# Feed-forward gate in seven products of quarters for each pair of blocks, on one Trainium2 core

## The chip, the cores and the metric

The kernel runs on one core of a Trainium2 chip, as one program. Its metric is the device time in microseconds of one execution, the median over repeated runs. Five engines work beside each other, each through its own instructions in order: TensorE (PE; its weight loads are listed as PEld), VectorE (DVE), ScalarE (ACT), GpSimd (POOL) and SyncE (SP), which issues the loads. They wait for each other by semaphores.

## What is computed

Two transformer layers (a mixer, an attention to a memory, a gated feed-forward) and then one hybrid layer, for 256 tokens of 2048 features, in float32. The change is in the feed-forward, which both of the first two layers run, with 5632 hidden features:

```python
def swiglu(h, w_gate, w_up, w_down):
    return (jax.nn.silu(h @ w_gate) * (h @ w_up)) @ w_down
...
        h = rms_norm(x, ffn_norm_g[l])
        x = x + swiglu(h, w_gate[l], w_up[l], w_down[l]).astype(x.dtype)
```

Beside the second layer's feed-forward the kernel sums w_ada, the weights that the hybrid layer's shift, scale and gate come from (`ada = c @ w_ada + b_ada`, one row c).

## The kernel before

Every long product keeps float32 precision by splitting both operands into a high and a low part: high·high + high·low + low·high, three matmuls on TensorE in place of one. The activations are split once and kept, as four pairs (xh, xl) of 512 features by 256 tokens. The weights come from DRAM in blocks of 128 x 1024 (512 KB: two chunks of 128 input features by 512 columns). For each, SyncE issues the load into one of five buffers `raw` (L410), ScalarE copies it to `wh` (L411, the high part), and VectorE subtracts that to give `wl` (L412). `wh` and `wl` have four buffers each (pool `wp`). These three instructions have a high priority, so the scheduler puts them ahead of other work of their engines, as early as buffers allow.

`block` (L401 and on) makes 256 tokens by 512 columns of a product: two PSUM banks `pw`, one for each half (m) of the tokens, out of four. A weight block serves twelve matmuls of 512 columns: two chunks, two halves of the tokens, three parts (L423 to L425). For the last weight block the products of the second half are held back until those of the first are done, so the first bank is finished earlier. TensorE's order is the order in which the program is written; that of the other engines comes from the scheduler. Other work (transposes of what comes next, attention heads) is cut into tasks, and `tick`, called between matmuls, lets each go on by a step.

The feed-forward (`ffn`) goes over 11 blocks of 512 hidden features. `hidden(j)` makes the gate block (L1186, 96 matmuls, then silu on ScalarE from the banks, L1188), the up block (96 matmuls), multiplies the two on VectorE (L1192), and spawns the task that transposes the result (L377) and splits it (L358, L359). `down(j - 1)` then multiplies the block before with w_down: four blocks of 24 matmuls, each added to the residual x by VectorE (L485, twice 512 columns). In layer two, `ada(9)` runs after each block: nine loads of w_ada (L1239) and nine multiply-and-sum instructions of 1024 columns on VectorE (L1240).

## Time and profile before

| | before |
|---|---|
| median of 3 runs | 3197.86 us (3197.11 to 3198.05) |
| span of the profiled execution, first to last instruction | 3196.7 us |
| TensorE busy in that span | 3175.3 us |
| VectorE busy | 2034.1 us |
| ScalarE busy | 1553.8 us |
| feed-forward of layer one, from the first issue of w_gate on | 428.7 us |
| feed-forward of layer two, last issue of w_down | 2340.1 us |

A busy TensorE row means that matmuls follow each other without a gap, since a matmul's end overlaps with the next one's start: the distance between starts is what one costs. Busy times of VectorE overlap in the same way by about a tenth of a microsecond when its instructions follow closely. An engine's share over the span is a mean over stages that differ, so the windows by stage count more than the page's first part.

### The profile page before, as it was taken

What the parts mean: (1) busy time and instruction counts of PE and PEld (TensorE: products, weight loads), DVE (VectorE), ACT (ScalarE), POOL (GpSimd) and SP (SyncE); (2) the same over time, 40 slices, a digit from 0 to 9 for tenths busy, and PEclk for the clock granted to TensorE, in tenths of its full rate; (3) what the DMA queues carried; (4) which work ended last, traced back from release to release, by engine and by line L of the source; (5) the groups of instructions that cost most, each with busy time, mean ns of one, the idle gap of its engine ahead of it and who ended that gap; (6) DMA issues with size and microseconds to landing.
All of it is one profiled execution on the core that took longest, in us unless ns stands there. A gap on an engine that the chain in (4) does not pass through costs nothing.

```text
span 3196.7 us, 41513 instructions
## 1 busy us (share of the span) xinstructions
PE 3175.3 (99%) x15705; PEld 2656.9 (83%) x15705; DVE 2034.1 (64%) x3015; ACT 1553.8 (49%) x2191; POOL 53.4 (2%) x77
## 2 busy tenths in 40 slices
PE   9999999999999999999999999999999999999998
PEld 8987888888888889887888888888878977888887
DVE  6886665555555566885767677766765555455554
ACT  7465564444444455474654444444454455444443
POOL 0010000000000000010000000000000000000000
PEclk9999999999999999999999999999999999999999
DMA  8554555555555556454567777777746533555454
GB/s 299 172 169 145 186 172 187 192 192 191 192 187 192 191 175 189 159 183 141 190 228 265 266 270 270 253 250 269 269 143 219 174 105 99 179 184 180 162 184 151
DMA packets 175160, 625.28 MB, mean 196 GB/s; under 512 B 19696, under 2 KB 19952, under 8 KB 174704
## 3 DMA queue, kind: packets, MB, share of 16 engines
q1 hardware_dynamic: 173952, 620.26, 58.2%
q8 instruction: 123, 2.02, 0.3%
q10 hardware_dynamic: 1008, 2.37, 0.2%
q14 instruction: 77, 0.63, 0.1%
HBM read 620.46 MB, written 2.10 MB: 195 GB/s over the span
## 4 chain that ended last, share of the span: by engine, by line
PE 96%; DVE 1%; DMA 1%; issue 1%; POOL 0%; ACT 0%; SPq 0%; DVEq 0%; POOLq 0%; ACTq 0%
PE pw L423 27%; PE pw L425 27%; PE pw L424 27%; PE pw L461 2%; PE pw L462 2%; PE pw L463 2%; PE mb L377 2%; PE mb L665 2%; DMA wada<-w_ada 1%; PE mb L1493 1%; PE mb L1346 0%; PE mb L903 0%; DVE wl L412 0%; PE mb L1496 0%; PE mb L887 0%
## 5 line engine op out<-in xcount | busy, mean ns | idle before, releaser
L412 DVE TENSOR_TENSOR wl<-raw,wh 128x1024 fp32r<-128x1024 f32 (+3 forms) x1069 | 1285.6, 1204 | 969.7 <-ACT wh L411 967.2
L411 ACT ACTIVATE wh<-raw 128x1024 fp32r<-128x1024 f32 (+3 forms) x1069 | 1114.9, 1043 | 1384.8 <-PE pw L425 1258.0
L423 PE MATMUL pw<-wh,xh 128*128 128x512 f32 (+2 forms) x3952 | 1555.4, 394 | 6.2 <-ACT wh L411 4.9
L425 PE MATMUL pw<-wh,xl 128*128 128x512 f32 (+2 forms) x3952 | 1526.3, 386 | 0.0
L424 PE MATMUL pw<-wl,xh 128*128 128x512 f32 (+2 forms) x3952 | 1524.6, 386 | 0.6 <-DVE wl L412 0.6
L423 PEld LDWEIGHTS pw<-wh,xh 128*128 128x128 f32 x3952 | 744.2, 188 | 153.3 <-ACT wh L411 4.9
L425 PEld LDWEIGHTS pw<-wh,xl 128*128 128x128 f32 x3952 | 743.1, 188 | 150.7 <-DVE xl L368 0.7
L424 PEld LDWEIGHTS pw<-wl,xh 128*128 128x128 f32 x3952 | 744.6, 188 | 141.6 <-DVE wl L412 2.1
L461 PE MATMUL pw<-xh,wh 128*128 128x256 f32 x640 | 183.2, 286 | 0.0
L463 PE MATMUL pw<-xh,wl 128*128 128x256 f32 x640 | 181.2, 283 | 0.0
L462 PE MATMUL pw<-xl,wh 128*128 128x256 f32 x640 | 181.1, 283 | 0.0
L485 DVE TENSOR_TENSOR x<-x,pw 128x512 f32<-128x512 f32 x224 | 144.9, 679 | 3.8 <-PE pw L425 3.8
L1240 DVE CUSTOM_DVE_ANT_0 wada<-wada,crow 128x1024 f32<-128x1024 f32 x96 | 117.3, 1221 | 33.9 <-DMA wada<-w_ada 33.8
L461 PEld LDWEIGHTS pw<-xh,wh 128*128 128x128 f32 x640 | 122.7, 192 | 1.3 <-issue 0.8
L462 PEld LDWEIGHTS pw<-xl,wh 128*128 128x128 f32 x640 | 122.8, 192 | 0.1
L463 PEld LDWEIGHTS pw<-xh,wl 128*128 128x128 f32 x640 | 122.7, 192 | 0.0
L630 ACT ACTIVATE t<-t,mn 128x256 f32<-128x256 f32 (+1 forms) x128 | 58.4, 457 | 63.1 <-DVE mn L627 62.3
L367 ACT ACTIVATE xh<-mb,par 128x256 fp32r<-128x256 f32 x112 | 50.9, 467 | 13.1 <-PE mb L377 12.2
L368 DVE SCALAR_TENSOR_TENSOR xl<-mb,par,xh 128x256 fp32r<-128x256 f32 x112 | 51.8, 478 | 3.7 <-ACT xh L367 2.6
L334 POOL TENSOR_TENSOR xr<-rs,mhalf 128x1 f32<-128x1 f32 x16 | 9.8, 619 | 2512.1 <-DVE rs L330 2306.4
L358 ACT ACTIVATE xh<-mb 128x512 fp32r<-128x512 f32 (+1 forms) x68 | 35.1, 516 | 30.5 <-PE mb L377 15.8
L627 DVE CUSTOM_DVE_ANT_0 t<-mb,cst 128x128 f32<-128x128 f32 x80 | 26.0, 354 | 25.8 <-PE mb L665 25.4
(358 smaller groups left out, 1564.4 us busy)
## 6 DMA issues: line engine op xcount, KB each, us to landing
raw<-w_gate SPq DMA_DIRECT2D x176, 512.0 KB, 3.6
raw<-w_up SPq DMA_DIRECT2D x176, 512.0 KB, 3.8
raw<-w_down SPq DMA_DIRECT2D x176, 512.0 KB, 3.6
raw<-w_out SPq DMA_DIRECT2D x96, 512.0 KB, 3.5
wada<-w_ada SPq DMA_DIRECT2D x96, 512.0 KB, 5.5
raw<-w_in_x SPq DMA_DIRECT2D x48, 512.0 KB, 3.9
raw<-w_in_z SPq DMA_DIRECT2D x32, 512.0 KB, 3.5
raw<-w_ma SPq DMA_DIRECT2D x32, 512.0 KB, 3.3
```

The costliest lines, as they stand in the source:

```text
L377: self.nc.tensor.transpose(t[:, j, m * P:(m + 1) * P], src(m), self.ident)
L411: nc.scalar.activation(h, raw, AF.Copy)
L412: nc.vector.tensor_tensor(l, raw, h.bitcast(F32), op=OP.subtract)
L423: nc.tensor.matmul(pt[m], lhsT=xh[:, k, ms], rhs=wh[:, j], start=c == 0, stop=False)
L424: nc.tensor.matmul(pt[m], lhsT=xh[:, k, ms], rhs=wl[:, j], start=False, stop=False)
L425: nc.tensor.matmul(pt[m], lhsT=xl[:, k, ms], rhs=wh[:, j], start=False, stop=c == 4 * n - 1)
L461: nc.tensor.matmul(pt, lhsT=h[:, j], rhs=xh[:, c], start=(k == 0), stop=False)
L462: nc.tensor.matmul(pt, lhsT=h[:, j], rhs=xl[:, c], start=False, stop=False)
L463: nc.tensor.matmul(pt, lhsT=l[:, j], rhs=xh[:, c], start=False, stop=(k == 15))
L485: self.nc.vector.tensor_tensor(xs, xs, pt[m], op=OP.add)
L665: nc.tensor.matmul(s[:, a:b], lhsT=q[:, m * P:(m + 1) * P], rhs=k[:, 0:b - a], start=(i == 0), stop=(i == len(parts) - 1))
L1240: nc.vector.tensor_tensor_reduce(out=t, in0=t, in1=self.crow[hf], scale=1.0, scalar=0.0, op0=OP.mult, op1=OP.add, accum_out=self.adap[:, j ...
```

## The change

Two gate blocks (1024 columns) are now made together. With the input h cut into quarters A11, A12, A21, A22 (first index the half of the tokens, second the half of the 2048 input features) and the weights of the two blocks into B11, B12, B21, B22 (first index the half of the input features, second the block), the four results need seven products of quarters in place of eight, in Winograd's form of Strassen's scheme: A11·B11, A12·B21, (A21+A22)·(B12-B11), (A11-A21)·(B22-B12), S2·T2 with S2 = A21+A22-A11 and T2 = B22-B12+B11, (A12-S2)·B22, and A22·(B21-T2).

- `x_sums` makes the four sums of input quarters once in each layer, on VectorE, and splits them into high and low (tiles fs): 28 instructions of 512 columns on VectorE and 8 copies on ScalarE.
- `gate_pair` is a task that goes on by one product at a time, beside up and down. A step takes a weight block of 512 KB (buffers fr, four of them), makes the weight sum on VectorE in place where one is needed (`combine`), splits it, and does six matmuls (two chunks, three parts, one half of the tokens). A pair has 28 steps, 16 weight sums and 28 loads: in the first half three loads for each quarter of the depth, in the second four, so that the blocks B11, B21 and B12 are loaded twice. The banks are one `pw` and three to four `mb`.
- In `ffn` five pairs are made in this way and the eleventh block as before. The gate of a pair is spawned first, then the two up blocks run, then down for the pair before, which now takes two blocks of the hidden features at once (four blocks of 48 matmuls, so half as many additions to x). With the last pair it takes three. The step's pace is one tick in the first pair and two in the others.
- up goes to a tile fu with the scale by ScalarE; the gate's four results come from the banks by ScalarE and VectorE, get silu, and are multiplied into fu.
- `ada(5)` runs after every up block in both layers, in the buffers fr.
- The pools of the other stages (sp, k2, k1) are closed at the start of the feed-forward and opened again at its last down, to make room for its own.

All comments and documentation strings are gone too, so the line numbers move: L410 to L412 become L423 to L425, L423 to L425 become L436 to L438, L377 becomes L390, L485 becomes L498, L1240 becomes L1401.

```diff
-        self.sp = pool("sp", NSLOT)
-        self.k2 = pool("k2", NT2)
-        self.k1 = pool("k1", NT1)
         self.sm = pool("sm", 1)
         self.psw = pool("psw", 4, space=PSUM)
         self.psm = pool("psm", 4, space=PSUM)
+        self.scope = ctx.enter_context(ExitStack())
+        self.open_main()
...
+    def part(self, **bufs):
+        self.scope.close()
+        for name, n in bufs.items():
+            setattr(self, name, self.scope.enter_context(self.tc.tile_pool(name=name, bufs=n, reuse_waits="tile")))
+    def open_main(self):
+        self.part(sp=NSLOT, k2=NT2, k1=NT1)
+    def open_ffn(self):
+        self.part(fs=8, fu=2, fe=4, fr=4, fc=2)
...
+    def half(self):
+        return self.fe.tile([P, 512], F32, name="fe", tag="fe")
+    def x_sums(self, pairs):
+        nc = self.nc
+        for t in pairs:
+            if isinstance(t, _Task):
+                yield from self.after(t)
+        prs = [self.get(t) for t in pairs]
+        S = [[self.fs.tile([P, 8, P], F32R, name="fs", tag="fs") for _ in range(2)] for _ in range(4)]
+        for i in range(2):
+            def quarter(k, m):
+                return [t[:, :, m * P:(m + 1) * P].bitcast(F32) for t in prs[2 * k + i]]
+            (h11, l11), (h12, l12), (h21, l21), (h22, l22) = (quarter(k, m) for m in range(2) for k in range(2))
+            def tmp():
+                return self.half().rearrange("p (a b) -> p a b", a=4)
+            def put(n, t):
+                h, l = (x[:, i * 4:i * 4 + 4] for x in S[n])
+                nc.scalar.activation(h, t, AF.Copy)
+                nc.vector.tensor_tensor(l, t, h.bitcast(F32), op=OP.subtract)
+            a, b = tmp(), tmp()
+            nc.vector.tensor_tensor(a, h21, h22, op=OP.add)
+            nc.vector.tensor_tensor(b, l21, l22, op=OP.add)
+            nc.vector.tensor_tensor(a, a, b, op=OP.add)
+            put(0, a)
+            nc.vector.tensor_tensor(b, a, h11, op=OP.subtract)
+            nc.vector.tensor_tensor(b, b, l11, op=OP.subtract)
+            put(1, b)
+            c = tmp()
+            nc.vector.tensor_tensor(c, h12, b, op=OP.subtract)
+            nc.vector.tensor_tensor(c, c, l12, op=OP.add)
+            put(3, c)
+            a, b = tmp(), tmp()
+            nc.vector.tensor_tensor(a, h11, h21, op=OP.subtract)
+            nc.vector.tensor_tensor(b, l11, l21, op=OP.subtract)
+            nc.vector.tensor_tensor(a, a, b, op=OP.add)
+            put(2, a)
+            yield 2
+        return S
+    def gate_pair(self, pairs, sums, srcs, r, u, pace):
+        nc = self.nc
+        S = yield from self.after(sums)
+        pr = [self.get(t) for t in pairs]
+        def quarter(k, m):
+            return lambda c: [t[:, c % 4, m * P:(m + 1) * P] for t in pr[2 * k + c // 4]]
+        def total(n):
+            return lambda c: [t[:, c] for t in S[n]]
+        def load(k, n, q):
+            t = self.fr.tile([P, 2, 512], F32, name="fr", tag="fr")
+            with self.early():
+                nc.sync.dma_start(t, srcs[n][2 * k + q // 2][q % 2])
+            return t
+        def combine(out, a, b, op):
+            with self.early():
+                nc.vector.tensor_tensor(out, a, b, op=op)
+        def product(bank, x, t, q, first, last):
+            with self.early():
+                h = self.wp.tile([P, 2, 512], F32R, name="wh", tag="wh")
+                l = self.wp.tile([P, 2, 512], F32R, name="wl", tag="wl")
+                nc.scalar.activation(h, t, AF.Copy)
+                nc.vector.tensor_tensor(l, t, h.bitcast(F32), op=OP.subtract)
+            for j in range(2):
+                xh, xl = x(2 * q + j)
+                g = not first
+                nc.tensor.matmul(bank, lhsT=xh, rhs=h[:, j], start=first and q == 0 and j == 0, stop=False,
+                                 skip_group_check=g)
+                nc.tensor.matmul(bank, lhsT=xh, rhs=l[:, j], start=False, stop=False, skip_group_check=g)
+                nc.tensor.matmul(bank, lhsT=xl, rhs=h[:, j], start=False, stop=last and q == 3 and j == 1,
+                                 skip_group_check=g)
+        def gated(t, n, m):
+            while len(u) <= n:
+                yield 1
+            with self.early():
+                nc.scalar.activation(t, t, AF.Silu, scale=r[:, m:m + 1])
+                nc.vector.tensor_tensor(u[n][:, m], u[n][:, m], t, op=OP.mult)
+        ba, bb, bd = self.wbank([P, 512]), self.bank([P, 512]), self.bank([P, 512])
+        for q in range(4):
+            w11, w21, w12 = load(0, 0, q), load(1, 0, q), load(0, 1, q)
+            product(ba, quarter(0, 0), w11, q, True, True)
+            yield pace
+            product(bb, quarter(1, 0), w21, q, True, True)
+            yield pace
+            combine(w12, w12, w11, OP.subtract)
+            product(bd, total(0), w12, q, True, True)
+            yield pace
+        with self.early():
+            t1, t5 = self.half(), self.half()
+            nc.scalar.activation(t1, ba, AF.Copy)
+            nc.vector.tensor_tensor(t1, t1, bb, op=OP.add)
+            nc.scalar.activation(t5, bd, AF.Copy)
+        yield from gated(t1, 0, 0)
+        bc, be = self.bank([P, 512]), self.bank([P, 512])
+        for q in range(4):
+            w12, w22, w11, w21 = load(0, 1, q), load(1, 1, q), load(0, 0, q), load(1, 0, q)
+            combine(w12, w22, w12, OP.subtract)
+            product(bc, total(2), w12, q, True, True)
+            yield pace
+            product(bd, total(3), w22, q, False, True)
+            yield pace
+            combine(w11, w12, w11, OP.add)
+            product(ba, total(1), w11, q, False, True)
+            yield pace
+            combine(w21, w21, w11, OP.subtract)
+            product(be, quarter(1, 1), w21, q, True, True)
+            yield pace
+        with self.early():
+            t2, t3 = self.half(), self.half()
+            nc.scalar.activation(t2, ba, AF.Copy)
+            nc.vector.tensor_tensor(t3, t2, bd, op=OP.add)
+            nc.vector.tensor_tensor(t2, t2, bc, op=OP.add)
+            nc.vector.tensor_tensor(t5, t2, t5, op=OP.add)
+            nc.vector.tensor_tensor(t2, t2, be, op=OP.add)
+        yield from gated(t3, 1, 0)
+        yield from gated(t5, 1, 1)
+        yield from gated(t2, 0, 1)
     def ffn(self, l, pairs, r):
         nc, I = self.nc, self.I
         parts = self.x_parts()
-        def hidden(j):
-            s = self.slot([P, 2, 512], "ff")
-            pt = self.block(pairs, I["w_gate"][l, j])
+        last = l == DEPTH - 1
+        self.open_ffn()
+        self.ada_start()
+        sums = self.spawn(self.x_sums(pairs), 1)
+        def up(j):
+            pt = self.block(pairs, I["w_up"][l, j])
+            s = self.fu.tile([P, 2, 512], F32, name="fu", tag="fu")
             for m in range(2):
-                nc.scalar.activation(s[:, m], pt[m], AF.Silu, scale=r[:, m:m + 1])
+                with self.early():
+                    nc.scalar.activation(s[:, m], pt[m], AF.Identity, scale=r[:, m:m + 1])
+            return s
+        def hidden(s, delay):
+            return self.spawn(self.transposed(lambda m: s[:, m]), delay)
+        def down(js, hs):
+            for nb in range(4):
+                self.x_add(nb, self.block(list(hs), [I["w_down"][l, nb, j] for j in js]))
+                self.tick()
+        prev = None
+        for p in range(NH_FFN // 2):
+            js = [2 * p, 2 * p + 1]
+            u = []
+            gate = self.spawn(self.gate_pair(pairs, sums, [I["w_gate"][l, j] for j in js], r, u, 2 if p else 1), 1)
+            for j in js:
+                u.append(up(j))
+                self.ada(5)
+            if prev is not None:
+                down(*prev)
+            self.get(gate)
+            prev = js, [hidden(s, 1 + 4 * i) for i, s in enumerate(u)]
+        j = NH_FFN - 1
+        s = up(j)
+        pt = self.block(pairs, I["w_gate"][l, j])
+        for m in range(2):
+            t = self.half()
+            with self.early():
+                nc.scalar.activation(t, pt[m], AF.Silu, scale=r[:, m:m + 1])
+                nc.vector.tensor_tensor(s[:, m], s[:, m], t, op=OP.mult)
+        js, hs = prev
+        js, hs = js + [j], hs + [hidden(s, 2)]
+        if last:
+            self.ada_end()
+        out = []
+        for nb in range(4):
+            pt = self.block(hs, [I["w_down"][l, nb, j] for j in js])
+            if nb == 0:
+                self.open_main()
+            if nb == 3:
+                with self.tc.high_priority(offset=2 * HP):
+                    self.x_add(nb, pt, parts)
+                    r = self.x_rms(parts)
+            else:
+                self.x_add(nb, pt, parts)
+            out.append(self.spawn(self.x_fm(nb), 2) if last else self.x_pair(nb, self.p(f"{l + 1}.attn_g")))
             self.tick()
-            pt = self.block(pairs, I["w_up"][l, j])
-            for m in range(2):
-                nc.vector.scalar_tensor_tensor(s[:, m], pt[m], r[:, m:m + 1], s[:, m], op0=OP.mult, op1=OP.mult)
-            return self.spawn(self.transposed(lambda m: s[:, m]), 2)
-        out = []
-        def down(j, h, end):
-            src = [h]
-            for nb in range(4):
-                pt = self.block(src, [I["w_down"][l, nb, j]])
-                if end and nb == 3:
-                    with self.tc.high_priority(offset=2 * HP):
-                        self.x_add(nb, pt, parts)
-                        r = self.x_rms(parts)
-                else:
-                    self.x_add(nb, pt, parts if end else None)
-                if end:
-                    out.append(self.x_pair(nb, self.p(f"{l + 1}.attn_g")) if l < DEPTH - 1
-                               else self.spawn(self.x_fm(nb), 2))
-                self.tick()
-            return r if end else None
-        prev = None
-        for j in range(NH_FFN):
-            h = hidden(j)
-            if prev is not None:
-                down(j - 1, prev, False)
-            self.ada(9)
-            prev = h
-        if l == DEPTH - 1:
-            self.ada_end()
-        return out, down(NH_FFN - 1, prev, True)
+        return out, r
     def ada_start(self):
         nc = self.nc
-        self.crow = [self.slot([P, 1024], "crow") for _ in range(2)]
+        self.crow = [self.fc.tile([P, 1024], F32, name="crow", tag="fc") for _ in range(2)]
         for i in range(2):
             nc.sync.dma_start(self.crow[i], self.I["c_rows"][:, i])
-        self.adap = self.one.tile([P, 48, 2], F32, name="adap")
-        self.ada_left = list(range(96))
     def ada(self, n):
         nc = self.nc
         for i in self.ada_left[:n]:
             j, hf = i // 2, i % 2
-            t = self.slot([P, 1024], "wada")
+            t = self.fr.tile([P, 1024], F32, name="fr", tag="fr")
             nc.sync.dma_start(t, self.I["w_ada"][j, :, hf])
...
     def run(self):
-        self.ada_left = []
+        self.adap = self.one.tile([P, 48, 2], F32, name="adap")
+        self.ada_left = list(range(96))
         pairs, r = self.start(), None
         for l in range(DEPTH):
             pairs, r, kt = self.mixer(l, pairs, r)
             pairs, r = self.cross(l, pairs, r, kt)
-            if l == DEPTH - 1:
-                self.ada_start()
             pairs, r = self.ffn(l, pairs, r)
         self.hybrid(pairs, r)
```

TensorE, at the start of the up product of the first pair in layer one (before: of the first gate block). The numbers are those of single tiles; pw and mb are banks, fs are sums of input quarters. Before:

```order
L424 MATMUL pw_4561<-wl_4656,xh_4511 128x512
L425 MATMUL pw_4561<-wh_4655,xl_4512 128x512
L423 MATMUL pw_4560<-wh_4673,xh_4511 128x512
L424 MATMUL pw_4560<-wl_4674,xh_4511 128x512
L425 MATMUL pw_4560<-wh_4673,xl_4512 128x512
```

Now:

```order
L436 MATMUL pw_4583<-wh_4750,xh_4512 128x512
L437 MATMUL pw_4583<-wl_4751,xh_4512 128x512
L438 MATMUL pw_4583<-wh_4750,xl_4513 128x512
L1270 MATMUL mb_4732<-wh_4778,fs_4640 128x512
L1272 MATMUL mb_4732<-wl_4779,fs_4640 128x512
L1273 MATMUL mb_4732<-wh_4778,fs_4641 128x512
```

Gate products of six matmuls, each with a weight block of its own, now stand between groups of six up matmuls.

VectorE, in layer one: before, near the end of an up block (xl is the low part of the transposed hidden block):

```order
L412 TENSOR_TENSOR wl_4908<-raw_4906,wh_4907 128x1024
L412 TENSOR_TENSOR wl_4933<-raw_4931,wh_4932 128x1024
L1192 SCALAR_TENSOR_TENSOR ff_4559<-pw_4728,xr_4549,ff_4559 128x512
L1192 SCALAR_TENSOR_TENSOR ff_4559<-pw_4729,xr_4549,ff_4559 128x512
L412 TENSOR_TENSOR wl_4951<-raw_4949,wh_4950 128x1024
```

Now, towards the end of the first pair (fr are gate weights or w_ada columns, adap their sums):

```order
L1259 TENSOR_TENSOR fr_5204<-fr_5206,fr_5204 128x1024
L1259 TENSOR_TENSOR fr_5208<-fr_5204,fr_5208 128x1024
L1266 TENSOR_TENSOR wl_5214<-fr_5204,wh_5213 128x1024
L1266 TENSOR_TENSOR wl_5230<-fr_5206,wh_5229 128x1024
L425 TENSOR_TENSOR wl_5241<-raw_5239,wh_5240 128x1024
L1259 TENSOR_TENSOR fr_5210<-fr_5210,fr_5208 128x1024
L1266 TENSOR_TENSOR wl_5253<-fr_5208,wh_5252 128x1024
L1401 ISA fr_5271,adap_93<-fr_5271,crow_4578 128x1024
L1401 ISA adap_93 128x1
L1266 TENSOR_TENSOR wl_5288<-fr_5210,wh_5287 128x1024
```

Sums of weights, splits of gate weights and w_ada's sums now stand between the splits of up weights.

SyncE, the loads of the same place. Before:

```order
L410 DMA raw_4708<-w_gate 128x1024
L410 DMA raw_4730<-w_up 128x1024
L410 DMA raw_4748<-w_up 128x1024
L410 DMA raw_4766<-w_up 128x1024
L410 DMA raw_4784<-w_up 128x1024
```

Now:

```order
L423 DMA raw_5192<-w_up 128x1024
L1254 DMA fr_5030<-w_gate 128x1024
L1254 DMA fr_5032<-w_gate 128x1024
L1254 DMA fr_5034<-w_gate 128x1024
L423 DMA raw_5239<-w_up 128x1024
L1254 DMA fr_5036<-w_gate 128x1024
```

Two to three loads into the four buffers fr now stand between two loads of up weights.

## Rows read from the trace of the kernel before

**Rows 1.** The page's first part: busy time, share and instructions of each engine.

```profile
PE 3175.3 (99%) x15705; PEld 2656.9 (83%) x15705; DVE 2034.1 (64%) x3015; ACT 1553.8 (49%) x2191; POOL 53.4 (2%) x77
```

**Rows 2.** Busy time by stretch: layer one, layer two, and two slices of it.

```profile
core 0: us, PE busy (x) PEld busy (x) DVE busy (x) ACT busy (x) POOL busy (x), PEclk, DMA share, GB/s
545.00:671.00 126.00, 126.00 (x565) 104.37 (x564) 69.15 (x68) 53.07 (x54) 0.00 (x0) 1.00 0.58 191
1680.00:1806.00 126.00, 126.00 (x567) 104.38 (x566) 93.27 (x112) 54.18 (x56) 0.00 (x0) 1.00 0.78 272
1720.00:1740.00 20.00, 20.00 (x94) 16.58 (x93) 18.91 (x26) 8.52 (x9) 0.00 (x0) 1.00 0.78 263
1740.00:1760.00 20.00, 20.00 (x90) 16.57 (x89) 10.60 (x10) 7.43 (x7) 0.00 (x0) 1.00 0.62 202
```

**Rows 3.** Timeline of TensorE in layer one: start, length, line, operation.

```profile
448.13 0.39 PE L424 MATMUL pw<-wl,xh 128*128 128x512 f32 x1
...
450.17 0.39 PE L424 MATMUL pw<-wl,xh 128*128 128x512 f32 x1
...
450.63 0.60 PE L377 MATMUL mb<-cst,x 128*128 128x128 f32 x4
450.98 0.48 PE L423 MATMUL pw<-wh,xh 128*128 128x512 f32 x1
```

**Rows 4.** Groups of VectorE by line and shape: count | busy us, mean ns | idle before.

```profile
L412 DVE TENSOR_TENSOR wl<-raw,wh 128x1024 fp32r<-128x1024 f32 x1019 | 1247.7, 1225 | 931.8 <-ACT wh L411 929.7
L1240 DVE CUSTOM_DVE_ANT_0 wada<-wada,crow 128x1024 f32<-128x1024 f32 x96 | 117.3, 1221 | 33.9 <-DMA wada<-w_ada 33.8
L368 DVE SCALAR_TENSOR_TENSOR xl<-mb,par,xh 128x256 fp32r<-128x256 f32 x112 | 51.8, 478 | 3.7 <-ACT xh L367 2.6
```

**Rows 5.** The same view of ScalarE: the copy of a weight block.

```profile
L411 ACT ACTIVATE wh<-raw 128x1024 fp32r<-128x1024 f32 x1019 | 1080.7, 1061 | 1348.2 <-PE pw L425 1225.4 <-PE pw L462 79.3 <-issue 35.2
```

**Rows 6.** Timeline of VectorE in layer two, instructions that follow without a gap.

```profile
1723.23 1.22 DVE L412 TENSOR_TENSOR wl<-raw,wh 128x1024 fp32r<-128x1024 f32 x1
1724.37 1.22 DVE L1240 CUSTOM_DVE_ANT_0 wada<-wada,crow 128x1024 f32<-128x1024 f32 x1
1725.51 0.08 DVE L1240 DVE_READ_ACCUMULATOR2_ANT adap<- 128x1 f32 x1
1725.51 1.22 DVE L412 TENSOR_TENSOR wl<-raw,wh 128x1024 fp32r<-128x1024 f32 x1
1726.65 1.28 DVE L359 TENSOR_TENSOR xl<-mb,xh 128x512 fp32r<-128x512 f32 x2
1727.85 1.27 DVE L485 TENSOR_TENSOR x<-x,pw 128x512 f32<-128x512 f32 x2
```

**Rows 7.** Waits in layer one, 440 to 1120 us: total us, times, longest.

```profile
ACT wh L411 <- PE pw L425: 369.1, 240, 1.7
DVE wl L412 <- ACT wh L411: 301.2, 236, 2.0
```

**Rows 8.** Loads issued from 600 to 700 us: count, KB, median us to landing.

```profile
raw<-w_gate SPq DMA_DIRECT2D x16, 512.0 KB, 3.5
```

**Rows 9.** Loads issued from 1650 to 1700 us, with w_ada.

```profile
wada<-w_ada SPq DMA_DIRECT2D x11, 512.0 KB, 5.2
...
raw<-w_gate SPq DMA_DIRECT2D x8, 512.0 KB, 4.6
```

**Rows 10.** Timeline of TensorE at the end of layer two's feed-forward.

```profile
2366.76 0.49 PE L745 MATMUL mb<-cst,xr 128*128 128x128 f32 x2
2368.76 0.49 PE L745 MATMUL mb<-cst,xr 128*128 128x128 f32 x2 [1.51 <-POOL xr L334]
2370.30 0.80 PE L423 MATMUL pw<-wh,xh 128*128 128x512 f32 x1 [1.05 <-ACT xh L1275]
...
2372.60 0.63 PE L425 MATMUL pw<-wh,xl 128*128 128x512 f32 x1
2373.03 0.63 PE L423 MATMUL pw<-wh,xh 128*128 128x512 f32 x1
```

## Prediction

> **What bounds the kernel now.** I read the page's busy times first, then stretches of the feed-forward stage, then single instructions. Over the span TensorE is busy 3175.3 of 3196.7 us and VectorE 2034.1 [rows 1], so the time is TensorE's own row of matmuls, and work taken off TensorE is worth its full length as long as the other engines keep up. Whether they do has to be read by stage [rows 2]: in layer one's feed-forward VectorE has 69.15 us of work in 126.00, in layer two's, where the w_ada columns are summed beside it, 93.27 in 126.00, and TensorE has no gap in either. In the 20 us from 1720 VectorE reaches 18.91 and TensorE still has 20.00, but the next 20 us ask only 10.60 of VectorE: a short excess is lent and given back. The prices: a 512-column matmul starts every 0.227 us (nine steps from 448.13 to 450.17), four transposes take 0.35 (450.63 to 450.98) [rows 3]. On VectorE an instruction of 1024 columns shows 1.225 or 1.221 us, one of 256 0.48 [rows 4]; back to back they start sooner than that: 1.14 us after a 1024 (1723.23, 1724.37, 1725.51), 0.60 after a 512 (two from 1726.65, the next at 1727.85) [rows 6]. ScalarE's copy of a weight takes 1.061 [rows 5].
>
> **What the change removes.** A pair of gate blocks falls from 192 to 168 matmuls, ten pairs in all, so 240 matmuls of 0.227 us: 54.5 us off TensorE. TensorE's listing of the changed program has just those 240 rows less, so the saving is really in it. If everything else stays hidden the time is 3197.9 - 54.5 = 3143.4. I set all sums against the profiled execution (span 3196.7) and give them on the median of 3197.86; the 1.2 us between them don't change.
>
> **What it adds.** A pair now splits 28 gate weights instead of 16 and makes 16 weight sums, all 1024-column VectorE instructions, and a layer makes 28 input-sum instructions of 512. In exchange the x additions fall from 16 to 8 in a pair, and w_ada moves from 18 to 10 columns a pair, but into both layers. A gate weight serves six matmuls (1.4 us of TensorE), where an up or down weight serves twelve (2.7). The first price is VectorE's row in two kinds of stretch.
>
> *Pairs two to five of a layer.* Between equal places of two pairs VectorE's listing has 86 instructions of 1024 (60 splits, 16 sums, 10 for w_ada) and 21 of 512: 86 x 1.14 + 21 x 0.60 = 110.6 us. TensorE has 552 matmuls and eight groups of transposes: 125.3 + 2.8 = 128.1. That is 86% for VectorE, between the 74% and the 95% of [rows 2], so on the whole it fits, with short clusters over the limit where ten w_ada sums stand close together.
>
> *The first pair of a layer.* Here there is no down work to spread the gate over: its products stand one behind every six up matmuls, the last five with no up work between them. From the split of the first gate weight to the third weight of the next up block VectorE's listing holds 71 instructions of 1024, 36 of 512 and 4 of 256: 80.9 + 21.6 + 1.9 = 104.4 us. TensorE between the same two points has 348 matmuls and two groups of transposes: 79.7. VectorE is 24.7 us short. What it may have done ahead is bounded by the four weight buffers: today ScalarE waits for TensorE to give a buffer back 240 times in layer one's stage, and VectorE for ScalarE 236 times [rows 7], so a weight is ready 1.061 + 1.225 = 2.3 us after the buffer came free at the earliest, and three others cover that time. Three are 4.1 us (all gate), 5.4 (two gate, one up) or 8.2 (all up): a lead of 1.8, 3.1 or 5.9 us. I take 3.1, since two of three weights there are gate's. TensorE so waits 21.6 us in the first pair of each layer (18.8 to 22.9), 43.2 in two layers. Nothing hides it, because TensorE's order is fixed: behind a waiting gate product stand the up matmuls, whose weights are split by the same VectorE.
>
> *Loads.* Gate weights and w_ada columns now come through four buffers fr instead of five raw ones, and 120 more loads of 512 KB are made. A load lands after 3.5 us at layer one's rate of 191 GB/s [rows 2, 8] and after 4.6 to 5.2 where w_ada runs beside it at 272 [rows 2, 9]; a pair will ask some 70 loads in 128 us, about 287 GB/s by the same count, so I take 5. By the buffers that the built program gives, about half of the first pair's 38 reloads have less than 5 us of VectorE work between the last reader of the buffer and the first of what is loaded into it (3.4 us often, 1.2 to 2.3 at the worst), and VectorE, in order, holds the splits of up weights behind a sum that waits for its load. No row of before shows this loop. Its bounds are 0 (the loads land in time) and 14 us a layer (every shortfall is paid one after another); I take 8, nearer to the middle, since several shortfalls run side by side. That is 16 in two layers. In pairs two to five VectorE has 17.5 us to spare, so most such waits are covered; 0 to 8 us a pair, and I take 2, nearer to zero because [rows 2] shows TensorE unhurt beside VectorE at 95%: 16 for eight pairs.
>
> *At nothing:* the down block of two inputs keeps its matmuls and saves 4.8 us of VectorE a pair, already counted; the last block of a layer is gated as before; ScalarE with 60 copies of 1.061 in 128.1 us has half its time left, and would cost only if VectorE's wait for it grew; the gate keeps one of four pw banks for a pair, and a block needs two, with the older block's first bank read while the held half of its products runs. The pools that are opened anew at the stage's start wait for readers that are done tens of matmuls earlier.
>
> **The sum:** -54.5 + 43.2 + 16 + 16 = +20.7, so 3197.9 + 20.7 = 3219 us, slower by 0.65%. With all low ends -54.5 + 37.6 = -16.9, 3181; with all high ends -54.5 + 45.8 + 28 + 64 = +83.3, 3281.
>
> **Rivals.** (a) *The buffers are never late.* Only VectorE's instruction count costs: -54.5 + 43.2, so 3187, down to 3181, and faster than before. For it: loads at 272 GB/s beside w_ada left no TensorE gap [rows 2]. Against it: there a buffer had twelve matmuls to be refilled in, and now often 3.4 us. The point that decides is 27.2 us of TensorE waiting a layer, all pairs together: below it the kernel is faster, above it slower. My terms give 21.6 + 8 + 8 = 37.6. (b) *All is hidden*, 3143: it needs VectorE to do 104.4 us of work in 79.7 with three buffers of lead, which no row supports. (c) *The fr loop binds in every pair*: 8 us in pairs two to five and 14 in the first, 3262 to 3281. Half of a pair's gate sums wait for a buffer, but VectorE's 17.5 us of slack speak against it. (d) *The clock falls.* At 2366.76 TensorE ran out of work, waited 1.51 and 1.05 us between matmuls, and the next thirteen start 0.43 us apart instead of 0.227 [rows 10], 2.6 us lost; at about twice 0.227 that is the 1.2 GHz level against 2.4. In a first pair the loss hides under VectorE's shortage; one fall in every one of ten pairs would add 26 us, 3245. The Trainium skill (TensorE: Matmul & The Clock Gate, section "HAM oscillation — how this bites in real kernels") says that TensorE, when it has to wait for data again and again between groups of matmuls, drops to the half rate each time and pays anew; here that rule speaks against the change and would give the 3245, and the one gap of this trace agrees with it. I leave the rule out of the sum, since most waits should be shorter than that gap.
>
> **Chances.** My forecast with its own range of 3192 to 3262: 0.54, of which 0.16 lies below 3204. Rival (a) 0.24, (b) 0.05, (c) 0.10, (d) with falls in most pairs 0.07, inside the forecast's range. About 0.2% is what a measurement here can tell from no change, 3191.5 to 3204.3. Faster: (a) + (b) = 0.29. Within: 0.16. Slower: 0.55. The range 3178 to 3264 holds the forecast, (d) and nearly all of (a), and leaves out (b), (c) and the rest: below 2 in 10.
>
> **What would show it.** In the first pair of each layer (some 80 us of matmuls from the first gate product) TensorE waits some 30 us in all, released by VectorE's split of a gate weight or of an up weight, with VectorE over 90% busy; VectorE's own idle time there ends on loads into fr. In pairs two to five TensorE is over 97% busy. Wrong would be: no TensorE gap in a first pair (the count or the lead is off), gaps that end on ScalarE or on a pw bank, a first pair as expected but waits of 8 us and more in each later one (then c), or matmuls at 0.43 us there (then d).

## The result and the profile after

The changed kernel takes 3349.95 us (3340.2 to 3350.7), the kernel before 3197.49 beside it: ratio 1.047, 95% interval 1.0456 to 1.0483. It is slower, as forecast, but by 152 us and not by 21, and outside the range.

The page's busy line of after, against [rows 1]:

```profile
PE 3195.2 (95%) x15465; PEld 2635.1 (79%) x15465; DVE 2350.5 (70%) x3305; ACT 1727.6 (52%) x2401; POOL 55.3 (2%) x77
```

240 matmuls are gone (15465 against 15705), and yet TensorE is busy 20 us longer and idle 152 us of its 3347.4 instead of 21. Layer one's feed-forward, first pair and the rest, in windows (window, then its length and the busy time of PE, PEld, DVE, ACT and POOL with instructions in brackets; then granted clock, DMA share, GB/s), first of before, then of after:

```profile
450.00:580.00 130.00, 130.00 (x591) 107.69 (x590) 72.51 (x78) 60.06 (x70) 1.11 (x2) 1.00 0.57 186
580.00:1200.00 620.00, 620.00 (x2787) 513.62 (x2786) 350.79 (x361) 269.55 (x292) 1.10 (x2) 1.00 0.58 189
```

```profile
450.00:580.00 130.00, 102.37 (x407) 79.87 (x406) 112.78 (x136) 65.21 (x81) 1.49 (x2) 0.88 0.68 230
580.00:1200.00 620.00, 576.75 (x2468) 463.26 (x2467) 474.36 (x486) 307.69 (x322) 0.00 (x0) 0.97 0.72 246
```

TensorE had no gap there before. Now it stands 27.6 us in the first pair and 43.3 after it, at a granted clock of 0.88 and 0.97. What it waits for in the second stretch (waiter, line, what ended the wait: us in total, times, longest):

```profile
PE mb L1270 <- ACT wh L1265: 21.5, 4, 6.4
PE pw L436 <- DVE x L498: 10.7, 7, 2.5
PE pw L437 <- DVE wl L425: 9.0, 13, 1.8
PE mb L1272 <- DVE wl L1266: 1.9, 4, 0.5
```

Four long waits and four of 2.5 us behind the x addition, one of each kind in each later pair. L1270 is the first matmul of a gate product, L1265 and L1266 are the copy and the split of its weight, L1259 the weight sum, L1254 its load, L1400 and L1401 a w_ada load and sum, L498 the x addition. The long wait of the second later pair, on SP's queue, VectorE, ScalarE and TensorE in turn (start, length, [idle before <- what ended it]):

```profile
775.22 0.33 SPq L1400 DMA_DIRECT2D fr<-w_ada  x1
...
779.23 0.33 SPq L1400 DMA_DIRECT2D fr<-w_ada  x1
...
781.51 1.47 SPq L1400 DMA_DIRECT2D fr<-w_ada  x2
787.54 1.46 SPq L423 DMA_DIRECT2D raw<-w_down  x2
789.05 0.42 SPq L1400 DMA_DIRECT2D fr<-w_ada  x1
789.82 7.35 SPq L1254 DMA_DIRECT2D fr<-w_gate  x4
```

```profile
785.14 1.23 DVE L1401 CUSTOM_DVE_ANT_0 fr<-fr,crow 128x1024 f32<-128x1024 f32 x1 [2.52 <-DMA fr<-w_ada]
...
795.58 1.23 DVE L1401 CUSTOM_DVE_ANT_0 fr<-fr,crow 128x1024 f32<-128x1024 f32 x1 [2.37 <-DMA fr<-w_ada]
796.73 0.08 DVE L1401 DVE_READ_ACCUMULATOR2_ANT adap<- 128x1 f32 x1
798.12 2.48 DVE L1259 TENSOR_TENSOR fr<-fr 128x1024 f32<-128x1024 f32 x2 [1.30 <-DMA fr<-w_gate]
```

```profile
799.43 1.06 ACT L1265 ACTIVATE wh<-fr 128x1024 fp32r<-128x1024 f32 x1 [8.37 <-DVE fr L1259]
```

```profile
800.54 0.80 PE L1270 MATMUL mb<-wh,fs 128*128 128x512 f32 x1 [4.76 <-ACT wh L1265]
801.80 0.80 PE L1272 MATMUL mb<-wl,fs 128*128 128x512 f32 x1 [0.46 <-DVE wl L1266]
802.40 0.63 PE L1273 MATMUL mb<-wh,fs 128*128 128x512 f32 x1
802.82 0.63 PE L1270 MATMUL mb<-wh,fs 128*128 128x512 f32 x1
```

Read it backwards. The product needs a weight sum, the sum a gate load, and the four gate loads are issued from 789.82 on, over 7.35 us, behind five w_ada loads. Each of those holds one of the four fr buffers until VectorE has summed it, and VectorE waits in front of the sum for the load. Behind the gap matmuls start 0.43 us apart, the 1.2 GHz level (granted clock 0.50), as in [rows 10]. The second kind of gap, 17 us later (TensorE, then VectorE):

```profile
814.58 0.39 PE L438 MATMUL pw<-wh,xl 128*128 128x512 f32 x1
817.49 0.50 PE L436 MATMUL pw<-wh,xh 128*128 128x512 f32 x1 [2.52 <-DVE x L498]
```

```profile
814.48 1.22 DVE L425 TENSOR_TENSOR wl<-raw,wh 128x1024 fp32r<-128x1024 f32 x1
815.62 1.22 DVE L1266 TENSOR_TENSOR wl<-fr,wh 128x1024 fp32r<-128x1024 f32 x1
816.75 0.68 DVE L498 TENSOR_TENSOR x<-x,pw 128x512 f32<-128x512 f32 x1
```

The next down block's first matmul waits for a pw bank, which the x addition frees, and that stands behind splits of higher priority, the last two of them shown.

### The profile page after: what moved, and what is told of

Same layout as the page of the kernel before. It is cut to its first block, busy times and chain, and to the rows that moved or that the text cites. A ratio compares the mean times of both kernels' runs of the same rounds, so it can differ in the third digit from the quotient of the medians.

```text
span 3347.4 us, 41830 instructions
## 1 busy us (share of the span) xinstructions
PE 3195.2 (95%) x15465; PEld 2635.1 (79%) x15465; DVE 2350.5 (70%) x3305; ACT 1727.6 (52%) x2401; POOL 55.3 (2%) x77
## 4 chain that ended last, share of the span: by engine, by line
PE 72%; DMA 11%; DVE 10%; issue 4%; ACT 2%; POOL 0%; DVEq 0%; SPq 0%; ACTq 0%; POOLq 0%
PE pw L436 18%; PE pw L438 17%; PE pw L437 17%; DMA fr<-w_gate 7%; DMA fr<-w_ada 3%; DVE wl L1266 3%; PE pw L474 2%; PE pw L476 2%; PE pw L475 2%; DVE wl L425 2%; PE mb L390 2%; DVE fr L1259 2%; PE mb L678 2%; PE mb L1272 2%; PE mb L1273 1%
## 5 line engine op out<-in xcount | busy, mean ns | idle before, releaser
L425 DVE TENSOR_TENSOR wl<-raw,wh 128x1024 fp32r<-128x1024 f32 (+3 forms) x909 | 1088.9, 1199 | 661.9 <-ACT wh L424 652.1
L424 ACT ACTIVATE wh<-raw 128x1024 fp32r<-128x1024 f32 (+3 forms) x909 | 943.9, 1039 | 1003.4 <-PE pw L438 595.7
L436 PE MATMUL pw<-wh,xh 128*128 128x512 f32 (+2 forms) x3312 | 1315.0, 397 | 26.6 <-DVE x L498 20.8
L437 PE MATMUL pw<-wl,xh 128*128 128x512 f32 (+2 forms) x3312 | 1284.5, 388 | 16.6 <-DVE wl L425 16.4
L438 PE MATMUL pw<-wh,xl 128*128 128x512 f32 (+2 forms) x3312 | 1282.5, 387 | 0.0
L436 PEld LDWEIGHTS pw<-wh,xh 128*128 128x128 f32 x3312 | 628.2, 190 | 159.6 <-DVE x L498 28.6
L438 PEld LDWEIGHTS pw<-wh,xl 128*128 128x128 f32 x3312 | 626.6, 189 | 128.5 <-DVE xl L381 0.7
L1265 ACT ACTIVATE wh<-fr 128x1024 fp32r<-128x1024 f32 x280 | 296.1, 1059 | 256.4 <-DVE fr L1259 126.5
L1266 DVE TENSOR_TENSOR wl<-fr,wh 128x1024 fp32r<-128x1024 f32 x280 | 341.1, 1221 | 31.9 <-ACT wh L1265 24.5
L1259 DVE TENSOR_TENSOR fr<-fr 128x1024 f32<-128x1024 f32 x160 | 195.6, 1223 | 70.9 <-DMA fr<-w_gate 70.4
L1401 DVE CUSTOM_DVE_ANT_0 fr<-fr,crow 128x1024 f32<-128x1024 f32 x96 | 117.3, 1222 | 64.5 <-DMA fr<-w_ada 64.3
L1270 PE MATMUL mb<-wh,fs 128*128 128x512 f32 x240 | 103.1, 429 | 56.9 <-ACT wh L1265 54.2
L1270 PEld LDWEIGHTS mb<-wh,fs 128*128 128x128 f32 x240 | 48.1, 200 | 72.5 <-ACT wh L1265 58.8
L1273 PE MATMUL mb<-wh,fs 128*128 128x512 f32 x240 | 100.8, 420 | 0.7 <-DVE fs L1216 0.7
```

Of the source, the lines that this page charges most:

```text
L424: nc.scalar.activation(h, raw, AF.Copy)
L425: nc.vector.tensor_tensor(l, raw, h.bitcast(F32), op=OP.subtract)
L436: nc.tensor.matmul(pt[m], lhsT=xh[:, k, ms], rhs=wh[:, j], start=c == 0, stop=False)
L437: nc.tensor.matmul(pt[m], lhsT=xh[:, k, ms], rhs=wl[:, j], start=False, stop=False)
L438: nc.tensor.matmul(pt[m], lhsT=xl[:, k, ms], rhs=wh[:, j], start=False, stop=c == 4 * n - 1)
L1259: nc.vector.tensor_tensor(out, a, b, op=op)
```

## The experiments

"Idle" is what TensorE's busy time leaves of the 130 us of 450 to 580 (first pair) and of the 620 of 580 to 1200, in windows as above; before 0.0 and 0.0.

| run | us | ratio to before, 95% | idle, first pair | idle, rest |
|---|---|---|---|---|
| after | 3349.95 | 1.0456 to 1.0483 | 27.6 | 43.3 |
| e1_no_ada | 3229.19 | 1.0082 to 1.0113 | 18.5 | 8.4 |
| e13_loads_only | 3330.22 | 1.0405 to 1.0433 | 23.8 | 41.7 |
| e14_sums_only | 3255.92 | 1.0171 to 1.0198 | 25.0 | 14.6 |
| e2_xadd_early | 3319.80 | 1.0367 to 1.0398 | 26.7 | 32.1 |
| e3_ada_raw | 3245.96 | 1.0142 to 1.0176 | 24.3 | 7.7 |
| e5_fr_spread | 3267.30 | 1.0201 to 1.0232 | 23.4 | 14.9 |
| e6_raw_bunch | 3268.60 | 1.0205 to 1.0236 | 20.2 | 17.3 |
| e7_hidden_late | 3237.02 | 1.0108 to 1.0138 | 21.1 | 6.1 |
| e11_no_sums | 3205.77 | 1.0013 to 1.0036 | 12.4 | 12.2 |
| e4_first_plain | 3192.75 | 0.9976 to 0.9995 | 2.4 | 5.4 |
| e8_even | 3241.66 | 1.0122 to 1.0156 | 4.4 | 17.7 |
| e9_ahead | 3232.32 | 1.0093 to 1.0124 | 5.2 | 17.4 |
| e12_two_plain | 3208.34 | 1.0020 to 1.0045 | 2.7 | 8.5 |
| e15_pool | 3341.12 | 1.0439 to 1.0468 | 22.5 | 35.1 |
| e18_own_row | 3191.37 | 0.9972 to 0.9989 | 0.2 | 5.3 |
| e19_offset | 3199.94 | 1.0000 to 1.0018 | 4.1 | 4.6 |

**The w_ada columns: loads or sums?** e1_no_ada drops both, the other two one of them each.

```diff
 t = self.fr.tile(...)                                    # e13 keeps these two lines,
 nc.sync.dma_start(t, self.I["w_ada"][j, :, hf])          # e14 drops them
-nc.vector.tensor_tensor_reduce(out=t, in0=t, in1=crow, ...)
+nc.vector.tensor_copy(adap[:, j, hf:hf + 1], t[:, 0:1])  # e13
+nc.vector.tensor_tensor(crow, crow, crow, op=OP.max)     # e14, with a copy of one column to adap
```

> The changed kernel without the w_ada columns: none of the 96 is loaded or summed (their sums are set to zero, so the output is not the reference's). It takes away 40 to 50 loads a layer through the four fr buffers, and as many sums of 1.14 us on VectorE. Theory 1 (a gate product starts late because its loads queue behind w_ada loads that wait for an fr buffer): the gap of 4.8 to 6.4 us ahead of the second stage of each later pair goes with the clock fall behind it (8 x 6.5 us), and the 7.9 us gap of the two first pairs too: 3350 - 68 = about 3280; the gap of 2.5 us behind the x addition stays. Rival, VectorE's count alone: only the first pairs gain, 2 x 10 x 1.14 = 23 us: 3327. Rival, the gap ends on the gate's own loads: 3340 to 3350.

> The changed kernel with the w_ada columns loaded through the four fr buffers as before, but VectorE only copies one element of each partition instead of summing the column (so the output is not the reference's). The loads, the buffers and VectorE's wait ahead of each stay; 96 x 1.14 = 109 us of VectorE's own time go. Theory L (the loads in the shared row of buffers and VectorE's wait for them cost the 121 us of e1_no_ada): 3315 to 3350. Theory C (VectorE's count): close to 3229, at most 3260.

> The changed kernel with each w_ada column's VectorE work replaced by an instruction of the same 1024 columns on a resident tile, and without any load or fr buffer for it (so the output is not the reference's). Theory L (loads and buffers): near e1_no_ada, 3229 to 3265, the rest being ten more instructions in the first pairs (2 x 10 x 1.14 = 23 us at most). Theory C (VectorE's count): 3320 to 3350. Both in the middle would say that the two add up.

Without the columns 121 us come back, far more than I had said. Their loads, with VectorE's wait for each of them, keep 101 of the 121 (3330 - 3229), the sums alone 27. TensorE's waits from 580 to 1200 of the run with loads only, then of the run with sums only:

```profile
PE mb L1270 <- ACT wh L1265: 22.2, 4, 6.2
PE pw L436 <- DVE x L498: 10.5, 6, 2.5
```

```profile
PE pw L436 <- DVE x L498: 12.7, 8, 4.4
PE mb L1272 <- DVE wl L1266: 1.8, 2, 1.7
```

The four long waits are the loads': in the first of the two VectorE is busy 435.5 us of this stretch instead of 474.4, and they stay. The second has none.

**The pw bank.**

```diff
-                self.x_add(nb, self.block(list(hs), ...))
+                pt = self.block(list(hs), ...)
+                with self.early():
+                    self.x_add(nb, pt)
```

> The changed kernel with one edit: the x additions of the down blocks stand on VectorE as early as the splits do (the same instructions). Theory 2 (with one of four pw banks kept by the gate, the next down block waits for the x addition of the block before, which stands behind splits on VectorE): the gap of 2.5 us at the second down block of each later pair goes, with the second fall of the clock behind it, 8 x (2.5 + 1.5) = 32 us: 3318. Rival (the gap only moves to the splits that now stand behind the addition): 3345 to 3350, and the gap there ends on VectorE's split.

3319.8, as theory 2 said. The wait that it removes, over the whole run, in after and in this run:

```profile
PE pw L436 <- DVE x L498: 20.8, 14, 2.5
```

```profile
PE pw L436 <- DVE x L498: 1.7, 3, 0.9
```

**Both, in an order that keeps the output; then each half of it.** All three keep e2's early x addition.

```diff
-                self.ada(5)                       # behind each up block
+        self.spawn(self.ada_spread(48, 3), 3)     # one column every third step (e3, e5)
-            t = self.fr.tile(...)
+            t = self.rawp.tile(...)               # e3, e6
```

> The same output by another order: the w_ada columns pass through the five raw buffers, one column at every third step of the blocks instead of five in a row through the four fr buffers, and the x additions stand early as in the run before. If theories 1 and 2 both hold and the raw buffers have room, the later pairs lose neither the 5 us nor the 2.5 us nor the clock: 3350 - 68 - 32 = 3250; the first pairs keep 20 to 30 us each. Rival, the loads are short of bandwidth or buffers wherever they pass: waits move to the raw loads and the time stays at 3310 or above.

> As e3_ada_raw (w_ada one column at every third step, early x additions), but the columns pass through the four fr buffers again. It tells apart the two edits of that run. Theory 1a (a w_ada load and a gate load in one row of four buffers is the trouble, however they are spaced): most of the loss of e2_xadd_early comes back, 3300 to 3320. Theory 1b (five columns in a row hold all four buffers, so that no gate load can be issued for as long as five of them take): spaced out they hold one at a time, and the time stays near 3246, at most 3260.

> As e2_xadd_early (five w_ada columns in a row behind each up block, early x additions), but the columns pass through the five raw buffers. Theory 1a (the shared row of four fr buffers): the gap ahead of the second stage of each later pair goes and the time falls from 3320 to 3245 to 3260. Theory 1b (five in a row are the trouble wherever they pass): the raw loads of the up and down weights wait in their place, each five columns hold all five raw buffers, and the time stays above 3280. Some gap at the raw loads is expected by both.

Both theories held: 3246. From 3320, spacing the columns alone gives 53 us and other buffers alone 51, both together 74. The long waits of layer one's later pairs, 22.1 us in e2, are 5.4 in e5 and gone in e6 and e3. So neither "the shared row" nor "five in a row" is the cause by itself: for most of the loss it takes five w_ada loads one behind the other in the row that the gate's next loads need. More than four fr buffers were not tried. e5 and e6 came out 7 to 9 us above what the theory that each confirms allowed.

**The first pair.** e7 moves the transposes that wait for the last gated result, e11 drops the input sums from e1, e4 gates the first pair in plain blocks.

```diff
-hidden(s, 1 + 4 * i)
+hidden(s, (1 if p else 8) + 4 * i)               # e7, on e3
-return lambda c: [t[:, c] for t in S[n]]
+return quarter(n // 2, n % 2)                    # e11, on e1; x_sums is not run
+if p < 1:                                        # e4, on e3
+    for j in js:
+        s, pt = up(j), self.block(pairs, I["w_gate"][l, j])
+        ...                                      # s *= silu(pt), as in the last block
+    down(*prev), if there is one; continue
```

> As e3_ada_raw with one edit: behind the first pair of a layer the transposes of its first hidden block stand seven steps later among the matmuls of the next up block. There TensorE waits 5.9 us in each layer for the last gated result, since in the first pair no down block runs between the last gate product and these transposes. Theory (a wait on the latency of the gating): 2 x 5.9 us and 1 to 3 us of half clock behind each go, 3246 - 15 = 3231. Rival (VectorE is behind there anyway, and the up block's splits take the wait over): 3240 to 3246, and the gap ends on VectorE's split.

> As e1_no_ada, and the gate's input sums are left out as well: the products that take them read a quarter of the input in their place (so the output is not the reference's); 28 VectorE instructions of 512 columns and 8 ScalarE copies a layer are missing, all in the first pair. It prices the first pair by VectorE's count: with w_ada and the sums out its work there is 104.4 - 11.4 - 16.8 = 76 us against TensorE's 79.7. Theory (the count is the cause of the first pair's loss, 28 us a layer in e1_no_ada): all of it goes but the wait of 7.7 us for the gated result ahead of the first hidden block, and its half clock: 3229 - 2 x 18 = 3193. Rival (the loss is the latency of loads, copies and gating): only the waits that end on the sums themselves go, 4 us a layer: 3221.

> The run before, with the first pair of each layer gated as two plain blocks (192 matmuls instead of 168) while the input sums are made; Strassen's products in pairs two to five alone. Theory (the first pair costs some 41 us of waiting a layer since its gate products have no down work between them, whatever the loads do): from the run before 2 x (41 - 24 x 0.227) = 71 us less if it keeps the whole loss, so some 3180; if spreading w_ada has already taken 10 to 15 us from each first pair, 40 to 50 us less. Rival (the waits move to the second pair, which then comes first): equal to the run before.

e7 gained 9 of the 15 us: its gap of 5.8 us went, and waits for splits took 2.4 of it over. e11 gained 23 where the count said 36 and latency 8. TensorE's waits of the first pair in after (first lines of the list), and the longest of them with VectorE's waits ahead of it:

```profile
PE mb L1270 <- ACT wh L1265: 8.7, 2, 7.9
PE mb L390 <- DVE fu L1281: 7.5, 1, 7.5
PE mb L1272 <- DVE wl L1266: 6.1, 4, 2.2
```

```profile
549.04 1.23 DVE L1401 CUSTOM_DVE_ANT_0 fr<-fr,crow 128x1024 f32<-128x1024 f32 x1 [1.77 <-DMA fr<-w_ada]
555.24 1.23 DVE L1259 TENSOR_TENSOR fr<-fr 128x1024 f32<-128x1024 f32 x1 [1.30 <-DMA fr<-w_gate]
557.66 0.80 PE L1270 MATMUL mb<-wh,fs 128*128 128x512 f32 x1 [7.92 <-ACT wh L1265]
```

The longest is the later pairs' wait again: a gate load behind five w_ada loads. Idle time there is 27.6 us in after, 23.8 with w_ada's loads and not its sums (e13), 25.0 with its sums and not its loads (e14), 18.5 without both (e1) and 12.4 without the input sums as well (e11), of which 7 to 8 are the wait for the gated result. So it does not simply go with VectorE's work: taking out the sums alone gives 3.8, and with the loads out the 7.9 go, but a wait for an input sum stands in their place, in both layers of e14:

```profile
PE mb L1270 <- ACT fs L1215: 16.5, 2, 8.4
```

e4 moved 53 us and is the first version below the kernel before.

**The places of the columns.** e8 was to improve e4 and lost 49 us by taking a column at every fifth step.

```diff
-self.spawn(self.ada_spread(48, 3), 3)
+self.spawn(self.ada_spread(48, 5), 3)            # e8 and e9, on e4
+self.spawn(self.ada_spread(48, 3), 5)            # e19, on e4
-self.ada(1); yield every
+dma_start(t, w_ada column), early; yield every; self.ada(1, t)   # e9, e12
-if p < 1:
+if p < 2:                                        # e12, e18, on e4
-t = self.rawp.tile(...)
+t = self.fr.tile(...)                            # e18
```

> As e4_first_plain (first pair in plain blocks, early x additions, w_ada through the raw buffers), with a w_ada column at every fifth step instead of every third, so that the 48 of a layer reach over nearly the whole stage. In e4_first_plain the gaps of a layer, 7 to 10 us, and half of its small delays lie in the first 280 us, where the columns are. If VectorE's bursts there are their cause, 5 to 8 us a layer come back: 3193 - 13 = 3180, faster than before by 0.5%. Rival (the bursts are the input sums' and the gate's own): 3190 to 3195.

> As e8_even with one edit: a w_ada column's load is issued with the weights' loads and its sum is made five steps later, so that VectorE finds it landed. In e8_even VectorE stood 41 times, 88.6 us in all, before a w_ada sum whose load had not landed, while the splits behind it in its row waited; in e4_first_plain 17 times, 15.1 us. The two differ by 49 us of time and by nothing but the places of the columns. Theory (VectorE, in order, waits for the load of a column, not for the sum's own 1.14 us): the waits go, 3242 falls to 3175 to 3190. Rival (a column over the whole stage costs its sum wherever it stands, or the raw buffer it now holds longer is missed): 3225 or more.

> Early x additions, w_ada through the raw buffers with its load issued three steps ahead of its sum, one column at every third step, and the first two pairs of a layer in plain blocks, where nearly all 48 columns of the layer then stand: Strassen's products are in pairs three to five alone. It saves 2 x 3 x 24 matmuls, 32.7 us. Theory (a pair without w_ada in it, without the input sums and with a down block beside it loses next to nothing): 3198 - 33 + 6 to 10 = 3171 to 3175. Rival (each such pair loses 2 to 3 us to splits even then): 3180 to 3185.

> The first two pairs of a layer in plain blocks, early x additions, one w_ada column at every third step as in e12_two_plain, but the columns pass through the four fr buffers, which the plain pairs do not use: a column's buffer was then left by the column four before it, some 12 steps ago, where in e12_two_plain the raw buffer that it takes was left by a weight's split 2 to 5 VectorE instructions before in 38 of 96 cases. Theory (a sum is late when fewer than 5 instructions of 1.14 us lie between the last reader of its buffer and itself, because the load takes 5 us): VectorE's waits for w_ada fall from 42 to under 10, and the time is 3198 - 33 + 6 to 12 = 3171 to 3177. Rival (the two added plain pairs lack bandwidth, whatever the buffers): 3200 to 3208.

> e4_first_plain with the w_ada columns two steps later (first column at step 5 instead of 3, still one in three). No column has fewer than 5 VectorE instructions between the last reader of its raw buffer and its sum, in this order as in that of e4_first_plain. Theory (the distance decides): within 6 us of e4_first_plain's 3193. Rival (the places of the columns among the gate's products decide, as chance has it): it moves by 15 us and more, as e8_even's places did.

VectorE's waits for w_ada over the run, of e4, e8, e9, e12, e18 and e19 in this order:

```profile
DVE raw L1423 <- DMA raw<-w_ada: 15.1, 17, 2.1
```

```profile
DVE raw L1423 <- DMA raw<-w_ada: 88.6, 41, 4.9
```

```profile
DVE raw L1428 <- DMA raw<-w_ada: 93.6, 43, 5.7
```

```profile
DVE raw L1428 <- DMA raw<-w_ada: 73.6, 42, 4.0
```

```profile
DVE fr L1423 <- DMA fr<-w_ada: 66.5, 55, 3.9
```

```profile
DVE raw L1423 <- DMA raw<-w_ada: 13.9, 16, 2.7
```

By the buffers of the built programs, the sum stands at most five VectorE instructions behind the last reader of its column's buffer (the accumulator's read of 0.08 us counts as one) for 0 of 96 columns in e4 and e19, 44 in e8, 46 in e9, 38 in e12. So e9's edit moved next to nothing: a load that is written earlier is still issued when its buffer comes free. That fits five of the six. It fails for e18, whose count is 0: there a w_ada load was issued 6.9 us before its sum and landed after 6.0 (medians; in e4 7.6 and 5.6), with 295 GB/s in the first pair, so VectorE waited all the same. It cost TensorE little, 5.5 us of idle time in layer one, in plain pairs, where a weight lasts twelve matmuls. The distance fits e8 against e4, but no run changed it alone and saw the waits go; a rule with a fixed landing time does not hold. Of the forecasts, e8 and e12 missed both of theirs, e18 lies between its two, and e19 is 7.2 us from e4, where the theory allowed 6 and its rival asked for 15.

**Is it VectorE's row?** e15 takes a column off VectorE altogether.

```diff
-nc.vector.tensor_tensor_reduce(out=t, in0=t, in1=crow, ..., accum_out=adap)
+nc.gpsimd.tensor_tensor(t, t, crow, op=OP.mult)
+nc.scalar.activation(t, t, AF.Copy, accum_out=adap)
```

> As e4_first_plain, but a w_ada column is multiplied on GpSimd and summed by ScalarE's accumulating copy, so that VectorE neither waits for its load nor spends 1.14 us on it; the loads and the raw buffers stay. Theory (what is left of the loss in the first 280 us of each stage, 10 us a layer of gaps and small delays, is VectorE's row): 3193 - 15 = 3178. Rival (the column holds a raw buffer longer, and GpSimd's use of memory slows VectorE's instructions beside it): 3193 or more; VectorE's 1024-column instructions would show longer than 1.22 us.

148 us worse than e4. ScalarE's waits in the run (one line of the list), and a stretch of ScalarE, GpSimd and VectorE:

```profile
ACT raw L1424 <- POOL raw L1423: 252.6, 83, 7.1
```

```profile
545.49 1.06 ACT L1424 ACTIVATE raw<-raw 128x1024 f32<-128x1024 f32 x1 [4.61 <-POOL raw L1423]
546.46 0.19 ACT L1424 ACTIVATION_READ_ACCUMULATOR raw<-raw 128x1 f32 x1
546.55 1.04 ACT L424 ACTIVATE wh<-raw 128x1024 fp32r<-128x1024 f32 x1
```

```profile
546.17 2.38 POOL L1423 TENSOR_TENSOR raw<-raw,crow 128x1024 f32<-128x1024 f32 x1 [0.71 <-DMA raw<-w_ada]
```

```profile
547.63 2.00 DVE L425 TENSOR_TENSOR wl<-raw,wh 128x1024 fp32r<-128x1024 f32 x1 [5.30 <-ACT wh L424]
550.71 1.23 DVE L425 TENSOR_TENSOR wl<-raw,wh 128x1024 fp32r<-128x1024 f32 x1 [1.08 <-ACT wh L424]
```

The wait for the column was not removed, it was handed to ScalarE: the accumulating copy stands in front of the weight copies, 83 times, 252.6 us. VectorE's split waits for those copies, and TensorE's largest wait is for the split:

```profile
PE pw L437 <- DVE wl L425: 62.2, 52, 4.4
```

So whether VectorE's row is what is left of e4's loss stays open.

## Why the prediction was wrong

**The saving** held: 240 matmuls less.

**The first pair** held in size, in part by luck. I had 21.6 us for VectorE's count and 8 for the loads, 29.6 a layer; TensorE's idle time is 27.6. But 7.9 of it are one wait behind five w_ada loads, the mechanism of the later pairs, and 7.5 the latency of the last gated result, which I had not seen. The count is part of the rest: without w_ada and the input sums 12.4 are left (e11). How the 27.6 divide between count and loads the runs do not say, since without w_ada's sums alone 23.8 are left (e13), and without its loads alone 25.0 (e14). VectorE is busy 87% there, not over 90.

**Pairs two to five** are the step that failed: "0 to 8 us a pair, and I take 2, nearer to zero because [rows 2] shows TensorE unhurt beside VectorE at 95%". The idle time is 10.8 us in each, and TensorE is busy 93%, not over 97. The argument compared VectorE's total with its time. But a wait in an in-order row is not filled by slack that comes later, and in [rows 2] w_ada went through slots that no weight used. Five w_ada loads now fill the row that the second stage's gate loads need, which costs some 5 us in each pair. Without w_ada the four pairs lose 8.4 us (e1), 2.1 each, and with its sums but not its loads 14.6 (e14), 3.7 each: the range held for a row that the gate has to itself. Rival (c) was nearest, for a reason that it did not give (and by its own terms its sum is 3273 to 3281, not from 3262 on).

**"The gate keeps one of four pw banks for a pair"**, put at nothing, failed too: 2.5 us in each later pair of layer one, 30 us of the time with all that hangs on it (e2). I had let the first bank be read while the held half of the products runs; the x addition that reads it came later, behind splits of higher priority.

**The clock** I priced rightly for one fall and left out. Summed over stretches of 2 us, TensorE's busy time times what the granted clock lacks of 1 is 24.5 us in layer one, in ten falls, and 22 in layer two, against 0.0 in layer one before. That is rival (d) on top of the forecast, with 19 falls for ten. All of layer one's gaps of 4.76 us and more have a fall at them or right behind; of the four of 2.5 us two do (817.49 and 1107.46) and two do not (676.51 and 963.10). In e4, where no wait of layer one is over 1.4 us, the same sum is 0.0. The Trainium skill (TensorE: Matmul & The Clock Gate, section "HAM oscillation — how this bites in real kernels") says that the slow clock is paid anew at each group of matmuls that has to wait for data. The trace agrees for the long gaps, not for each short one.

Three of the prediction's own signs of being wrong came: gaps that end on ScalarE's copy and on a pw bank, more than 8 us in each later pair, and matmuls at 0.43 us there.

Layer one, then: 35 us too little in the later pairs (43.3 for 8), 24.5 for the clock, 2 too much in the first pair, and a remainder of 14, where matmuls start a little over 0.227 us apart: 72 of the 131 us that I missed by; the rest is layer two's. What the steps of the remainder wait for is not shown.

What stays open: in e4 and e18 TensorE's idle time is down to 5 to 8 us a layer, the saving is 44 and 33 us, and the kernel gains 5 and 6 us. Some 8 to 11 us a layer are in such steps; what makes them long was not tried.

## What to carry to other kernels

Before an operand stream is put through a buffer row that others use, look who frees each buffer and what stands before that instruction in its engine's order; a consumer that waits for a late load stops everything behind it on its engine (here VectorE, and ScalarE in e15), and average slack does not pay that back. A stream with no hurry (w_ada) should enter one at a time and never as a run as long as the row, and freeing instructions (the x addition) should rank with those that feed TensorE. With plain first pairs, so that the seven products stand only where a down block runs beside them, the kernel is faster than before by 0.2% (e18) and 0.15% (e4), the best that these runs found. No run has all pairs plain beside the other changes (half as many x additions, for one), so how much of that the products give is not shown.

## What was not expected of the hardware

GpSimd's multiply of 128x1024 takes 2.38 us in the row of e15 shown, and the VectorE split that meets it shows 2.00 us instead of 1.23. The Trainium skill (SBUF — State Buffer, section "Who interferes with whom") says that a VectorE instruction with two SBUF inputs, as the split is, contends with a GpSimd instruction that reads SBUF, and that the lock is exclusive. The trace agrees: the split of 547.63 ends at 549.63, 1.1 us after GpSimd's instruction at 548.55.
